# Second layer's modulation moved beside the first feed-forward part, neighbourhood output product between the memory heads, and one split path of probabilities

## The chip, the cores and the metric

The kernel runs on one core of a Trainium2 chip. The metric is the device time of one execution in microseconds (us). Several executions give a median. One execution is also recorded by the hardware profiler, and every duration read below comes from that one.

## What is computed

Two blocks run one after the other on 512 tokens of width 1024, in 32-bit arithmetic. The first mixes three branches (a retention, a neighbourhood attention over an 8 x 64 grid, and a cross attention to 256 memory rows), each gated by a sigmoid of a projection, and ends in a hierarchical mixture of experts. Only the parts that the change touches:

```python
def _memory_cross_attention(xq, mem_n, w_kv):
    mk, mv = jnp.split(mem_n @ w_kv, 2, axis=-1)
    ...
    sc = jnp.einsum('bshd,bmhd->bhsm', q, k).astype(jnp.float32) * (XA_HEAD_DIM ** -0.5)
    p = jax.nn.softmax(sc, axis=-1).astype(v.dtype)
    return jnp.einsum('bhsm,bmhd->bshd', p, v).reshape(b, s, XA_WIDTH)
```

The second block has two layers of attention (latent, differential and grouped heads) and a gated feed-forward part (`silu(h @ gate) * (h @ up) @ down`, inner width 2816). Each layer is modulated: shift, scale and gate are a product of `silu(c)` of two conditioning vectors with a matrix w_ada of 6 x 1024 columns per layer, plus a bias.

## The kernel before, in words

**Precision and weights.** A 32-bit product is made of three products in a rounded format (mm3, lines 97 to 101): high by high, high by low, low by high. A weight tile of 1 MB is loaded by the sync engine's queue (SP) into a tile "raw" of 128 x 2048 (line 70), of which there are NRAW = 3, shared by all that is loaded so. ACT copies it into whi (line 81), DVE subtracts that from raw into wlo (line 82); NW = 3 such pairs exist. `W` does load and split; `ahead` calls it early and keeps the pair. All DMAs of weights stand in SP's queue in program order, and a load waits there until what last read its raw buffer is done.

**The modulation, ada() (lines 1260 to 1327).** A generator over both layers, three rounds each. A round begins with a bias row, loaded into a raw buffer and multiplied by ones; then eight tiles of w_ada follow. Each is loaded into a raw buffer, and four matmuls (32 x 512 outputs, line 1301) read it straight from there, without split. Then come an ACT copy, four transposes and a copy by DVE. `bg()` (line 1329) takes one step of it: it is called after every projection of the first block, in the attention's pairs and after the output products, so that both layers' modulation is done by 658 us.

**First block.** Projections, retention, then the neighbourhood attention in 16 pairs (`pairs`, line 613): scores of two pairs ahead, probabilities turned on PE (prt), product with the values. In the last pairs `ahead` fetches the next weights. `branch_out` (line 491) then makes the branch's output: for each of four 256-wide column groups g a projection to the gate (24 matmuls per half, prj), the product with the branch's output weights (bo), and the gated sum into mixT. For the neighbourhood branch memory_keys runs in the middle of it (mkp, mvp). Then come the memory heads, `pairs` with n = 8 (xs scores, prt turns, xpo products), with a step of ada after each, and their branch_out.

**Attention of the second block (`pipeline`, line 1865).** In 20 units per layer of scores, softmax, turns and products. `turned` transposes normalized probabilities on PE into a PSUM bank tp (three banks of that name) and splits the bank in a high and a low part. SPLITS = (1, 0, 1, 0, 1, 0, 1) says which path each part takes. Path 0: ACT copies from PSUM into pehi, DVE subtracts from PSUM into pelo (line 92). Path 1: ACT copies from PSUM into pe, which is one of the raw buffers for the length of the attention; DVE casts pe to pehi (line 1939), GpSimd subtracts into pelo (line 1940). With six token tiles (layer 0) a unit has seven parts, four on path 1; with four tiles (layer 1) six parts, three on path 1.

**Output projection and feed-forward part.** `attn_out` (line 2002) holds one PSUM bank for each token tile in its first products. `ffn` (line 2055) has 11 groups of inner columns. For each it loads f_gate and f_up, makes 96 products of 512 and, in layer 0, 96 of 256 columns (fg), lets ACT and DVE form the hidden rows (hh, hl), then loads f_down of the group before (`weight(g - 1)`) and makes 72 products (fd) in layer 0, each added by DVE to acc. Layer 0 has six token tiles, layer 1 four.

Of the kernel before, what the change touches and what calls it, by code (L numbers as in the profile page):

```python
# [8 lines left out]
F = mybir.dt.float32  # L9
# [28 lines left out]
class Kern:  # L38
    def __init__(self, tc, ins, outs, stop=None):
        self.tc = tc  # L40
        self.nc = tc.nc
        self.i = ins
        self.o = outs
        self.stop = stop
        self.es = ExitStack()
        self.early = {}


# [138 lines left out]
    def build(self):  # L187
        tc, nc = self.tc, self.nc
        es = self.es
        self.NRAW, self.NW = 3, 3  # L190
        self.cp = es.enter_context(self.pool("consts"))
        self.wp = es.enter_context(self.pool("weights"))
        self.beside = self.ada()
        self.NT5 = 6
        with self.pool("work1") as self.work, self.psum(7, own=dict(ada=1)):
            self.first_block()
            self.bg(100)
# [106 lines left out]
    def proj_b(self, g, evac, after=lambda t: None, before=()):  # L304

        wh, wl = self.w_in(g)

        def product(t):
            p = self.mm("prj")[:, :256]
            for kt in range(8):  # L310
                self.mm3(p, self.h(0, kt, t * 128, t * 128 + 128), self.h(1, kt, t * 128, t * 128 + 128),
                         wh[:, kt], wl[:, kt], kt == 0, kt == 7)
            evac(t, p)

        self.skew(4, *before, product, after)
        self.bg()

# [19 lines left out]
    def retention(self):  # L337
# [108 lines left out]

        nc.sync.dma_start(diff, self.i["posdiff"])
        values(0)
        scores(0)
# [40 lines left out]

    def branch_out(self, yT, nk, wname, gate_group, first=False, middle=lambda: None):

        nc = self.nc
        nw = 2048 // nk
        w = None
        for g in range(4):
            if g == 2:
                middle()
            if g * 256 % nw == 0:
                w = self.W(self.i[wname][g * 256 // nw, 0], k=nk)  # L500

            def evac(f, p, g=g, w=w):
                mx = self.mixT[:, 2 * g + f]
                gt = self.t5("gate")
                nc.scalar.activation(gt, p, AF.Tanh, scale=0.5)
                nc.vector.tensor_scalar(gt, gt, 1.0, 0.5, op0=OP.add, op1=OP.mult)
                py = self.mm("bo")
# [9 lines left out]
            self.proj_a(gate_group + g, evac)  # L517

# [19 lines left out]
    def neighbourhood(self):  # L538
# [53 lines left out]

        self.pairs(16, scores, values, ("w_na_o", (0, 0), 4), ("w_in", (24, 0), 8), ("w_in", (25, 0), 8))
# [4 lines left out]
        oT = self.rows_to_T(o[:, ::-1])  # L598
        self.branch_out(oT, 4, "w_na_o", 24, middle=lambda: self.memory_keys(rows))

# [11 lines left out]

    def pairs(self, n, scores, values, *chunks):

# [4 lines left out]
        for i in range(n + 1):  # L619
# [17 lines left out]
            if i % 2 or n == 8:  # L637
                self.bg()

# [53 lines left out]
    def memory_attention(self):  # L693
# [28 lines left out]

        self.pairs(8, scores, values, ("w_xa_o", (0, 0), 4), ("w_in", (28, 0), 8), ("w_in", (29, 0), 8))
        if self.stop == "xa":
# [535 lines left out]
    def ada(self):  # L1260
# [27 lines left out]
        for l in range(2):  # L1288
# [34 lines left out]
            for nm, g, at in (("a", "g_attn_pre", 8), ("f", "g_ffn_pre", 32)):  # L1323
                t = cp.tile([128, 8, 2], F, name="pre_%s%d" % (nm, l))
                nc.vector.tensor_scalar(t, md[:, at:at + 8], 1.0, None, op0=OP.add)
                nc.vector.tensor_tensor(t, t, self.vec(g, 8 * l, 8)[:, :, None].to_broadcast([128, 8, 2]), op=OP.mult)
                self.preA[nm, l] = t

    def bg(self, n=1):

        for _ in range(n):
            next(self.beside, None)

# [422 lines left out]
    def attention(self, l, yB, ap, nq):  # L1756
# [12 lines left out]
        raw = self.wp.tile([128, 4, 512], F, name="pe", tag="raw", bufs=self.NRAW)  # L1769
        self.copies = [raw[:, j] for j in range(4)]  # L1770

# [87 lines left out]

    SPLITS = (1, 0, 1, 0, 1, 0, 1)
    LAG = 5

    def pipeline(self, units, nq, ap):
# [56 lines left out]
        def turned(u):  # L1922
# [79 lines left out]
    def attn_out(self, l, yB, hT, hp, nq):  # L2002
# [23 lines left out]
        w = weight(0)  # L2026
        ps = [self.mm("wo")[:, :256] for _ in range(nq)]
        for kt in range(8):
            for t in range(nq):
                mms(ps[t], w, t, kt)  # L2030
        for t in range(nq):
# [23 lines left out]
    def ffn(self, l, hT, hp, nq):  # L2055
# [24 lines left out]
        with self.pool("f_w") as fp:  # L2080
            hids, begun = [], []
            for g in range(11):
# [5 lines left out]
                for c0 in range(0, T, N):  # L2088
# [12 lines left out]
                    for f in range(2):  # L2101
# [5 lines left out]
                        self.split(hh[:, c], hl[:, c], sg)  # L2107
                hids.append(hid)
                if 0 < g < 10:
                    wd = weight(g - 1)  # L2110
                    for t in range(nq):
                        down(t, [(hids[g - 1], wd)])
                    begun.append(g)

            parts = [(hids[g], weight(g)) for g in (9, 10)]
# [138 lines left out]
```

## Time and profile before

| | |
|---|---|
| median of 3 executions | 3010.52 us (2999.06 to 3013.27) |
| the profiled execution | 3001.12 us |
| its span (first to last instruction) | 2999.3 us |
| mean granted TensorE clock | 0.975 of full speed |
| PE busy | 2852.1 us |
| DVE busy | 1768.6 us |
| ACT busy | 1296.2 us |
| POOL busy | 413.1 us |

PE is TensorE's matmuls, PEld its weight loads, DVE VectorE, ACT ScalarE, POOL GpSimd, SP the engine that issues the DMAs of weights. Busy time is time in which an instruction of the engine runs. A wait is the engine's idle time ahead of an instruction, put down to what released that instruction last. The time of an execution is the span and some 2 us around it.

### The profile page before, as it was taken

What the parts mean: (1) busy time and instruction counts of PE and PEld (TensorE: products, weight loads), DVE (VectorE), ACT (ScalarE), POOL (GpSimd) and SP (SyncE); (2) the same over time, 40 slices, a digit from 0 to 9 for tenths busy, and PEclk for the clock granted to TensorE, in tenths of its full rate; (3) what the DMA queues carried; (4) which work ended last, traced back from release to release, by engine and by line L of the source; (5) the groups of instructions that cost most, each with busy time, mean ns of one, the idle gap of its engine ahead of it and who ended that gap; (6) DMA issues with size and microseconds to landing.
All of it is one profiled execution on the core that took longest, in us unless ns stands there. A gap on an engine that the chain in (4) does not pass through costs nothing. (4 is left out here: it accounts for less than half of the span.)

```text
span 2999.3 us, 44707 instructions
## 1 busy us (share of the span) xinstructions
PE 2852.1 (95%) x17896; PEld 2463.1 (82%) x17896; DVE 1768.6 (59%) x3239; ACT 1296.2 (43%) x2275; POOL 413.1 (14%) x430
## 2 busy tenths in 40 slices
PE   8999999999799988999999999999988999899998
PEld 6997777769788878887789888888788777888887
DVE  6653344346588877789857343434565787644445
ACT  3222243234477765388745111212342787432222
POOL 2200010000110023156410000000010454000000
PEclk9999999999899999999999999999989999899999
DMA  5443464364799972421013121211233310322221
GB/s 201 141 145 138 150 207 161 142 225 168 262 388 385 351 275 87 146 78 27 4 71 141 71 71 56 71 57 71 77 127 101 106 24 3 141 99 105 92 98 71
DMA packets 130084, 399.78 MB, mean 133 GB/s; under 512 B 62199, under 2 KB 74887, under 8 KB 93128
## 3 DMA queue, kind: packets, MB, share of 16 engines
q1 hardware_dynamic: 116206, 350.04, 32.7%
q0 software_dynamic: 13520, 46.55, 4.6%
q8 instruction: 143, 2.34, 0.3%
q14 instruction: 71, 0.58, 0.1%
q10 hardware_dynamic: 144, 0.26, 0.0%
HBM read 356.64 MB, written 39.39 MB: 132 GB/s over the span
## 5 line engine op out<-in xcount | busy, mean ns | idle before, releaser
L82 DVE TENSOR_TENSOR wlo<-raw,whi 128x2048 fp32r<-128x2048 f32 (+2 forms) x203 | 421.2, 2077 | 292.9 <-ACT whi L81 292.4
L81 ACT ACTIVATE whi<-raw 128x2048 fp32r<-128x2048 f32 (+2 forms) x203 | 351.4, 1739 | 493.7 <-PE fd L101 128.6
L101 PE MATMUL fg<-hT,wlo 128*128 128x512 f32 (+1 forms) x1120 | 386.4, 345 | 0.0
L100 PE MATMUL fg<-hT,whi 128*128 128x512 f32 (+1 forms) x1120 | 386.2, 345 | 0.0
L99 PE MATMUL fg<-hT,whi 128*128 128x512 f32 (+1 forms) x1120 | 386.2, 345 | 0.0
L99 PEld LDWEIGHTS fg<-hT,whi 128*128 128x128 f32 x1120 | 211.1, 189 | 29.3
L100 PEld LDWEIGHTS fg<-hT,whi 128*128 128x128 f32 x1120 | 210.7, 188 | 29.3
L101 PEld LDWEIGHTS fg<-hT,wlo 128*128 128x128 f32 x1120 | 210.8, 188 | 29.0
L1940 POOL TENSOR_TENSOR pelo<-pe,pehi 128x512 fp32r<-128x512 f32 x140 | 181.4, 1298 | 192.0 <-DVE pehi L1939 187.5
L2106 DVE TENSOR_TENSOR sg<-sg,fg 128x512 f32<-128x512 f32 (+1 forms) x70 | 40.1, 573 | 282.1 <-PE fg L101 282.1
L101 PE MATMUL fd<-whi,hl 128*128 128x512 f32 x440 | 173.2, 394 | 0.0
L100 PE MATMUL fd<-wlo,hh 128*128 128x512 f32 x440 | 172.5, 392 | 0.0
L99 PE MATMUL fd<-whi,hh 128*128 128x512 f32 x440 | 171.2, 389 | 0.0
L1903 DVE TENSOR_REDUCE smx<-sn 128x1 f32<-128x768 f32 x160 | 151.8, 950 | 19.1 <-PE sn L1897 18.3
L2073 DVE TENSOR_TENSOR acc<-acc,fd 128x512 f32<-128x512 f32 x180 | 120.8, 686 | 65.1 <-PE fd L101 65.1
L131 PE MATMUL tp<-ident,pn 128*128 128x128 f32 x960 | 150.8, 276 | 4.1 <-DVE pelo L92 2.8
L1906 ACT ACTIVATE pn<-sn,smx 128x768 f32<-128x768 f32 x160 | 144.0, 905 | 19.7 <-DVE smx L1903 16.1
L99 PE MATMUL eg<-whi,xt 128*96 128x256 f32 x512 | 147.0, 287 | 0.0
L100 PE MATMUL eg<-wlo,xt 128*96 128x256 f32 x512 | 145.1, 283 | 1.5 <-DVE wlo L82 1.5
L101 PE MATMUL eg<-whi,xt 128*96 128x256 f32 x512 | 144.9, 283 | 0.0
L82 DVE TENSOR_TENSOR wlo<-rawx,whi 128x2048 fp32r<-128x2048 f32 x58 | 133.0, 2292 | 20.0 <-ACT whi L81 20.0
L1955 PE MATMUL pv<-pehi,vp 128*128 128x512 f32 (+1 forms) x280 | 124.3, 447 | 8.7 <-ACT oT L1959 7.8
(658 smaller groups left out, 7552.0 us busy)
## 6 DMA issues: line engine op xcount, KB each, us to landing
raw<-in_w_in SPq DMA_DIRECT2D x53, 1024.0 KB, 5.3
raw<-in_w_ada SPq DMA_DIRECT2D x48, 1024.0 KB, 5.1
raw<-in_f_gate SPq DMA_DIRECT2D x22, 1024.0 KB, 4.8
raw<-in_f_up SPq DMA_DIRECT2D x22, 1024.0 KB, 4.8
raw<-in_f_down SPq DMA_DIRECT2D x22, 1024.0 KB, 4.8
rawx<-in_e_gate SPq DMA_DIRECT2D x19, 1024.0 KB, 9.1
rawx<-in_e_up SPq DMA_DIRECT2D x19, 1024.0 KB, 9.0
rawx<-in_e_down SPq DMA_DIRECT2D x18, 1024.0 KB, 8.6
```

The source lines that it names most:

```text
L81: keep(nc.scalar.activation(hi[:, c], raw[:, c], AF.Copy))
L82: keep((eng or nc.vector).tensor_tensor(lo[:, c], raw[:, c], hi[:, c].bitcast(F), op=OP.subtract))
L99: t.matmul(ps, lh, rh, start=first, stop=False)
L100: t.matmul(ps, lh, rl, start=False, stop=False)
L101: t.matmul(ps, ll, rh, start=False, stop=last)
L131: self.nc.tensor.transpose(out, in_, self.ident[:k, :k])
L1903: nc.vector.tensor_reduce(m[:, t:t + 1], p[:, :768], axis=AX.X, op=OP.max, negate=True)
L1906: nc.scalar.activation(P[t], p[:, :768], AF.Exp, bias=m[:, t:t + 1], accum_out=su[:, t:t + 1])
L1940: nc.gpsimd.tensor_tensor(el, e, eh.bitcast(F), op=OP.subtract)
L1955: nc.tensor.matmul(p, v[:, k + a], e[:, a * N:a * N + N], start=k == k0 and a == 0 and e is eh, stop=k + a == 5 and e is el)
L2073: nc.vector.tensor_tensor(acc[:, t, cs], acc[:, t, cs], p, op=OP.add)
L2106: nc.vector.tensor_tensor(sg, sg, pp[1], op=OP.mult)
```

## The change

It does five things.

- Layer 1's part of ada() leaves the first block. `bg` counts down from 26 steps, which is layer 0's part, and then does nothing until `second` is set, at layer 0's output projection. In layer 0's ffn two steps follow the products of every even group and three those of every odd one, ahead of f_down's weight; what is left runs after the last group. The products have a PSUM bank of their own, ada, for which the other products' banks go from six to five.
- bg is no longer called in the first projections.
- `branch_out` becomes a generator, branch_steps. The neighbourhood branch's output product is run in 16 steps, two after each of the memory heads' pairs; memory_keys goes ahead of it; the weights fetched in the neighbourhood pairs are w_mem_kv.
- All parts of the probabilities take path 0. pe no longer holds a raw buffer.
- attn_out's first products hold two token tiles in one PSUM bank.

```diff
+    def branch_steps(self, yT, nk, wname, gate_group, first=False):
...
+            wg = self.w_in(gate_group + g)
+            for f in range(2):
+                p = self.mm("prj")
...
+                    self.mm3(p, wg[0][:, kt, fs], wg[1][:, kt, fs], self.h(0, kt), self.h(1, kt), kt == 0, kt == 7)
...
+                yield
+                if f == 1 and g < 3:
+                    self.ahead(("w_in", (gate_group + g + 1, 0), 8))
...
-        self.branch_out(oT, 4, "w_na_o", 24, middle=lambda: self.memory_keys(rows))
+        self.na_out = self.branch_steps(self.rows_to_T(o[:, ::-1]), 4, "w_na_o", 24)
+        self.memory_keys(rows)
...
+        def beside(i):
+            for _ in range(2):
+                next(self.na_out, None)
...
-                with self.pool("l_h") as hp, self.psum(6, own=dict(trp=2)):
+                self.second = True
+                with self.pool("l_h") as hp, self.psum(6 - (l == 0), own=dict(trp=2, ada=1)):
...
         for _ in range(n):
-            next(self.beside, None)
+            if self.layer0 > 0 or self.second:
+                self.layer0 -= 1
+                next(self.beside, None)
...
-                    if self.SPLITS[6 if t0 else k]:
-                        e = self.copies[0]
-                        self.copies.append(self.copies.pop(0))
-                        nc.scalar.activation(e, p, AF.Copy)
-                        nc.vector.tensor_copy(eh, e)
-                        nc.gpsimd.tensor_tensor(el, e, eh.bitcast(F), op=OP.subtract)
-                    else:
-                        self.split(eh, el, p)
+                    self.split(eh, el, p)
...
-        ps = [self.mm("wo")[:, :256] for _ in range(nq)]
+        banks = [self.mm("wo").rearrange("p (a n) -> p a n", a=2) for _ in range(nq // 2)]
+        ps = [banks[t // 2][:, t % 2] for t in range(nq)]
...
+                if l == 0:
+                    self.bg(3 if g % 2 else 2)
                 if 0 < g < 10:
                     wd = weight(g - 1)
```

Three places show how instructions move. Line numbers below 100 are one higher in the changed kernel; its ada loads stand on lines 1319 (bias) and 1324, its products on 1326.

SP's queue in layer 0's feed-forward part, from f_gate of group 1 on, with what each load waits for (a number behind an engine's name is a semaphore's; DMAHW are earlier transfers); before:

```order
L70 DMA raw<-in_f_gate 128x2048 [waits DMAHW4_49,DMAHW6_49,DVE_49,Activation_49]
L70 DMA raw<-in_f_up 128x2048 [waits DMAHW7_49,DVE_49,PE_49]
L70 DMA raw<-in_f_down 128x2048 [waits DMAHW6_49,DMAHW0_49,DVE_49]
L70 DMA raw<-in_f_gate 128x2048 [waits DMAHW1_49,DVE_49,PE_49]
L70 DMA raw<-in_f_up 128x2048 [waits DMAHW7_49,DMAHW2_49,DVE_49]
L70 DMA raw<-in_f_down 128x2048 [waits DMAHW3_49,DMAHW0_49,DVE_49]
L70 DMA raw<-in_f_gate 128x2048 [waits DMAHW1_49,DVE_49]
```

The same place with the change:

```order
L71 DMA raw<-in_f_gate 128x2048 [waits DMAHW6_49,DMAHW3_49,PE_49]
L71 DMA raw<-in_f_up 128x2048 [waits DMAHW7_49,DMAHW4_49,PE_49]
L1324 DMA raw<-in_w_ada 128x2048 [waits DMAHW5_49,DMAHW0_49,PE_49]
L1324 DMA raw<-in_w_ada 128x2048 [waits DMAHW6_49,DVE_49]
L1324 DMA raw<-in_w_ada 128x2048 [waits DMAHW7_49,DMAHW2_49,DVE_49]
L71 DMA raw<-in_f_down 128x2048 [waits DMAHW0_49,PE_49]
L71 DMA raw<-in_f_gate 128x2048 [waits DMAHW1_49,PE_49]
L71 DMA raw<-in_f_up 128x2048 [waits DMAHW2_49,PE_49]
L1324 DMA raw<-in_w_ada 128x2048 [waits DMAHW3_49,DVE_49]
L1324 DMA raw<-in_w_ada 128x2048 [waits DMAHW4_49,DVE_49]
L71 DMA raw<-in_f_down 128x2048 [waits DMAHW5_49,DVE_49]
L71 DMA raw<-in_f_gate 128x2048 [waits DMAHW0_49,DVE_49]
```

Between f_up of a group and f_down of the one before it now stand two or three loads of w_ada, and the first f_down waits for PE.

PE in the same part, at the end of group 1's products, before:

```order
L99 MATMUL fg<-hT_15686,whi 128x256
L100 MATMUL fg<-hT_15687,whi 128x256
L101 MATMUL fg<-hT_15686,wlo 128x256
L99 MATMUL fd<-whi,hh 128x512
L100 MATMUL fd<-wlo,hh 128x512
L101 MATMUL fd<-whi,hl 128x512
```

With the change:

```order
L100 MATMUL fg<-hT_15394,whi 128x256
L101 MATMUL fg<-hT_15395,whi 128x256
L102 MATMUL fg<-hT_15394,wlo 128x256
L1326 MATMUL ada<-raw,silu_c 32x512 x12
L100 MATMUL fd<-whi,hh 128x512 x5
L101 MATMUL fd<-wlo,hh 128x512
L102 MATMUL fd<-whi,hl 128x512
```

Three steps' twelve matmuls stand ahead of f_down's products, of which five with whi now come first.

PE in the memory heads (xs scores, prt turned probabilities, xpo products), before:

```order
L99 MATMUL xs<-mk,xqh 128x256
L100 MATMUL xs<-mk,xqh 128x256
L101 MATMUL xs<-mk,xql 128x256
L131 MATMUL prt<-ident,xpr 128x128 x4
L1301 MATMUL ada<-raw,silu_c 32x512 x3
L719 MATMUL xpo<-mv,prT 128x128 x4
```

With the change:

```order
L102 MATMUL bo<-oTh,wlo 128x512
L100 MATMUL xs<-mk,xqh 128x256
L101 MATMUL xs<-mk,xqh 128x256
L102 MATMUL xs<-mk,xql 128x256
L132 MATMUL prt<-ident,xpr 128x128 x4
L736 MATMUL xpo<-mv,prT 128x128 x4
L100 MATMUL prj<-hTh,whi 128x512
L101 MATMUL prj<-hTl,whi 128x512
L102 MATMUL prj<-hTh,wlo 128x512
```

In place of a step of ada, 24 gate products (prj) and 12 output products (bo) now stand between the heads' pairs.

## Rows read from the trace of the kernel before

**Rows 1.** The page: span, and busy time, share and instructions of each engine.

```profile
span 2999.3 us, 44707 instructions
PE 2852.1 (95%) x17896; PEld 2463.1 (82%) x17896; DVE 1768.6 (59%) x3239; ACT 1296.2 (43%) x2275; POOL 413.1 (14%) x430
```

**Rows 2.** Windows by stage; columns stand in the first row.

```profile
core 0: us, PE busy (x) PEld busy (x) DVE busy (x) ACT busy (x) POOL busy (x), PEclk, DMA share, GB/s
415.00:458.00 43.00, 40.16 (x240) 28.25 (x240) 24.19 (x81) 24.41 (x58) 5.96 (x12) 0.81 0.81 288
584.00:618.00 34.00, 29.83 (x226) 20.57 (x222) 20.52 (x41) 19.92 (x48) 3.57 (x7) 1.00 0.73 263
1290.00:1532.00 242.00, 221.24 (x1530) 190.40 (x1529) 204.03 (x330) 196.36 (x450) 128.00 (x109) 0.99 0.12 34
1660.00:2166.00 506.00, 505.99 (x2685) 431.23 (x2684) 205.09 (x314) 106.49 (x142) 1.59 (x3) 1.00 0.18 62
2335.00:2556.00 221.00, 207.34 (x1332) 169.64 (x1330) 184.68 (x318) 176.21 (x357) 107.17 (x97) 0.99 0.18 48
```

**Rows 3.** Tile ada in 415 to 662 us: records, min/median/max ns, first and last start.

```profile
L1301 PE MATMUL ada<-raw,silu_c x192: 592/617/1062, 420.2 to 656.0; 128*32 128x512 f32 x192
L1296 PE MATMUL ada<-raw,ones x24: 587/600/612, 419.2 to 600.3; 1*32 1x512 f32 x24
L131 PE MATMUL ada<-ident,adar x13: 271/272/273, 414.8 to 658.4; 128*128 128x128 f32 x13
```

**Rows 4.** Timeline, 509.5 to 512 us: start, duration, engine, line, operation.

```profile
509.61 1.06 PE L1296 MATMUL ada<-raw,ones 1*32 1x512 f32 x8
510.60 1.07 PE L1301 MATMUL ada<-raw,silu_c 128*32 128x512 f32 x8
```

**Rows 5.** Waits of PE, 415 to 584 us: in total, times, longest us.

```profile
PE mvp L100 <- DVE wlo L82: 1.5, 1, 1.5
```

**Rows 6.** Waits of PE, 584 to 618 us.

```profile
PE ada L1301 <- DMA raw<-in_w_ada: 4.2, 3, 2.6
```

**Rows 7.** DMA issues, 1660 to 2166 us: KB each, median us to landing.

```profile
raw<-in_f_down SPq DMA_DIRECT2D x9, 1024.0 KB, 4.8
```

**Rows 8.** Groups of ACT and DVE, 1660 to 2166 us: count, busy us, mean ns, idle before.

```profile
L81 ACT ACTIVATE whi<-raw 128x2048 fp32r<-128x2048 f32 x28 | 53.8, 1920 | 149.9 <-PE fd L101 128.6 <-PE fg L100 21.4
L82 DVE TENSOR_TENSOR wlo<-raw,whi 128x2048 fp32r<-128x2048 f32 x28 | 64.1, 2290 | 42.9 <-ACT whi L81 42.9
```

**Rows 9.** Timeline of PE, 1733 to 1735 us: down products.

```profile
1733.75 0.39 PE L99 MATMUL fd<-whi,hh 128*128 128x512 f32 x1
1733.98 0.39 PE L100 MATMUL fd<-wlo,hh 128*128 128x512 f32 x1
```

**Rows 10.** Waits of PE, 1660 to 2180 us.

```profile
PE prj L99 <- ACT whi L81: 5.2, 1, 5.2
```

**Rows 11.** Windows behind that wait; columns as in rows 2.

```profile
2172.00:2174.00 2.00, 1.56 (x7) 1.56 (x8) 0.69 (x1) 1.94 (x4) 0.00 (x0) 0.51 0.06 27
2174.00:2176.00 2.00, 2.00 (x13) 2.00 (x12) 0.94 (x4) 1.48 (x5) 1.56 (x3) 0.64 0.00 0
```

**Rows 12.** Groups of DVE: 1290 to 1532 us first, then 2335 to 2556 us.

```profile
L1939 DVE CAST pehi<-pe 128x512 fp32r<-128x512 f32 x75 | 45.1, 608 | 6.5 <-ACT pe L1938 5.9
L92 DVE TENSOR_TENSOR pelo<-tp,pehi 128x512 fp32r<-128x512 f32 x56 | 38.1, 680 | 2.2 <-ACT pehi L91 2.1
...
L1939 DVE CAST pehi<-pe 128x512 fp32r<-128x512 f32 x60 | 28.1, 468 | 5.8 <-ACT pe L1938 5.2
L92 DVE TENSOR_TENSOR pelo<-tp,pehi 128x512 fp32r<-128x512 f32 x60 | 41.0, 684 | 2.1 <-ACT pehi L91 1.2
```

**Rows 13.** Waits of PE, 1290 to 1532 us.

```profile
PE tp L129 <- DVE pelo L92: 3.3, 3, 1.4
PE tp L131 <- DVE pelo L92: 2.8, 4, 1.0
PE tp L1968 <- DVE pelo L92: 0.8, 2, 0.6
```

More of the change, by code (lines that the diff above doesn't have):

```diff
@@ L46, in __init__ @@
         self.early = {}
+        self.first = True
     def pool(self, name, bufs=1, space=None):
@@ L193, in build @@
         self.beside = self.ada()
+        self.layer0, self.second = 26, False
         self.NT5 = 6
@@ L196, in build @@
             self.first_block()
-            self.bg(100)
+            self.bg(self.layer0)
         if self.stop is None or self.stop[:2] in ("at", "ao", "fo"):
@@ L315, in proj_b @@
         self.skew(4, *before, product, after)
-        self.bg()
+        if not before and not self.first:
+            self.bg()
     def proj_a(self, g, evac):
@@ L447, in retention @@
         nc.sync.dma_start(diff, self.i["posdiff"])
+        self.first = False
         values(0)
@@ L489, in branch_rows, with branch_out @@
         return self.mix[:, 4:6].rearrange("p a (b c) -> p (a b) c", b=2)
-    def branch_out(self, yT, nk, wname, gate_group, first=False, middle=lambda: None):
+    def branch_out(self, *args, **more):
+        for _ in self.branch_steps(*args, **more):
+            pass
+    def branch_steps(self, yT, nk, wname, gate_group, first=False):
         nc = self.nc
@@ L496, in branch_out @@
         for g in range(4):
-            if g == 2:
-                middle()
             if g * 256 % nw == 0:
                 w = self.W(self.i[wname][g * 256 // nw, 0], k=nk)
-            def evac(f, p, g=g, w=w):
-                mx = self.mixT[:, 2 * g + f]
+            wg = self.w_in(gate_group + g)
+            for f in range(2):
+                p = self.mm("prj")
+                fs = slice(f * 128, f * 128 + 128)
+                for kt in range(8):
+                    self.mm3(p, wg[0][:, kt, fs], wg[1][:, kt, fs], self.h(0, kt), self.h(1, kt), kt == 0, kt == 7)
                 gt = self.t5("gate")
@@ L506, in evac @@
                 nc.vector.tensor_scalar(gt, gt, 1.0, 0.5, op0=OP.add, op1=OP.mult)
+                yield
+                if f == 1 and g < 3:
+                    self.ahead(("w_in", (gate_group + g + 1, 0), 8))
+                mx = self.mixT[:, 2 * g + f]
                 py = self.mm("bo")
@@ L516, in evac @@
                     nc.vector.tensor_tensor(mx, mx, gt, op=OP.add)
-            self.proj_a(gate_group + g, evac)
+                yield
+            self.bg()
     def na_table(self):
@@ L591, in values @@
                                     rec[:, :, None].to_broadcast([128, 2, 64]), op=OP.mult)
-        self.pairs(16, scores, values, ("w_na_o", (0, 0), 4), ("w_in", (24, 0), 8), ("w_in", (25, 0), 8))
+        def beside(i):
+            if i % 2:
+                self.bg()
+        self.pairs(16, scores, values, beside, ("w_mem_kv", (0, 0), 8), ("w_mem_kv", (1, 0), 8), ("w_mem_kv", (2, 0), 8))
         if self.stop == "na":
@@ L611, in exps, with pairs @@
         return rec
-    def pairs(self, n, scores, values, *chunks):
+    def pairs(self, n, scores, values, beside, *chunks):
         nc = self.nc
@@ L636, in pairs @@
                 chunks = chunks[1:]
-            if i % 2 or n == 8:
-                self.bg()
+            beside(i)
     def rows_to_T(self, o):
@@ L721, in values, with beside @@
                                     rec[:, :, None].to_broadcast([128, 2, 128]), op=OP.mult)
-        self.pairs(8, scores, values, ("w_xa_o", (0, 0), 4), ("w_in", (28, 0), 8), ("w_in", (29, 0), 8))
+        def beside(i):
+            for _ in range(2):
+                next(self.na_out, None)
+        self.pairs(8, scores, values, beside)
+        for _ in self.na_out:
+            pass
+        self.ahead(("w_xa_o", (0, 0), 4), ("w_in", (28, 0), 8))
         if self.stop == "xa":
@@ L1327, in ada @@
                 self.preA[nm, l] = t
+            yield
     def bg(self, n=1):
         for _ in range(n):
-            next(self.beside, None)
+            if self.layer0 > 0 or self.second:
+                self.layer0 -= 1
+                next(self.beside, None)
     def gates(self, l, which, nq, pool):
@@ L1768, in attention @@
             self.pairs8 += [(hi[:, j], lo[:, j]) for j in range(4)]
-        raw = self.wp.tile([128, 4, 512], F, name="pe", tag="raw", bufs=self.NRAW)
-        self.copies = [raw[:, j] for j in range(4)]
         self.fold = ap.tile([128, 64], F, name="fold")
@@ L1858, in attention @@
             nc.vector.tensor_tensor(y, y, gd[:, None, :].to_broadcast([128, 4, 64]), op=OP.mult)
-    SPLITS = (1, 0, 1, 0, 1, 0, 1)
     LAG = 5
@@ L2026, in attn_out @@
         w = weight(0)
-        ps = [self.mm("wo")[:, :256] for _ in range(nq)]
+        banks = [self.mm("wo").rearrange("p (a n) -> p a n", a=2) for _ in range(nq // 2)]
+        ps = [banks[t // 2][:, t % 2] for t in range(nq)]
         for kt in range(8):
             for t in range(nq):
-                mms(ps[t], w, t, kt)
+                ts = slice(t * 128, t * 128 + 128)
+                for i, (a, b) in enumerate(((0, 0), (0, 1), (1, 0))):
+                    nc.tensor.matmul(ps[t], hT[a][:, kt, ts], w[b][:, kt], start=kt == 0 and t % 2 == 0 and i == 0,
+                                     stop=kt == 7 and i == 2, skip_group_check=True)
         for t in range(nq):
@@ L2113, in ffn @@
                     begun.append(g)
+            if l == 0:
+                self.bg(100)
             parts = [(hids[g], weight(g)) for g in (9, 10)]
```

1 line of the change is left out of this document (removed).

## The prediction

> **What bounds the kernel now.** I read the page's engine shares first [rows 1]: TensorE (PE) is busy 2852.1 of 2999.3 us, 95%, VectorE (DVE) 59%, ScalarE (ACT) 43%, GpSimd (POOL) 14%. So the whole kernel can gain at most some 147 us of PE's idle time and what the clock takes, and work moved from one dense stretch of PE to another costs there what it saves here.
>
> Then the table by stage [rows 2]. Its lines are the stretches on which a term rests: the end of the neighbourhood pairs (415 to 458 us), the memory heads (584 to 618), layer 0's attention (1290 to 1532), layer 0's feed-forward part (1660 to 2166) and layer 1's attention (2335 to 2556). The reader is to see where PE has gaps: 2.84 us in the first (43.00 less 40.16), 4.17 in the second, 20.8 and 13.7 in the attentions. The feed-forward part, which receives the moved work, has none: 505.99 busy of 506.00 us, at DMA share 0.18.
>
> **The second layer's modulation: what leaves.** In 415 to 662 us lie 192 records of modulation products and 24 of bias products [rows 3]. The timeline shows a call's four matmuls as eight records, and the distance from one call to the next [rows 4]: 509.61 to 510.60 and 510.60 to 511.59, so 0.99 us. That makes 24 calls and 3 biases: 27 x 0.99 = 26.7 us; with 12 transposes of about 0.15 (estimate: they overlap, one alone is 0.27 [rows 3]) 28.5 us leave. In the tail of the pairs the calls also filled gaps; I let 2.9 us of the gain be lost there, about as much as is idle now [rows 2]. With the calls go their waits on w_ada, 4.2 us in the memory heads [rows 6], and, as the keys' weights are now fetched ahead, the 1.5 us of the product mvp [rows 5]. **First block: -28.5 + 2.9 - 4.2 - 1.5 = -31.3 us.**
>
> **Where it arrives.** The same 28.5 us are put between products that have no gap: **+28.5**.
>
> **What its loads push.** This is the term that decides. A weight tile lands in one of three raw buffers, is copied by ACT (whi), subtracted by DVE (wlo), and then multiplied. Before, each load waits for a split alone (the SP rows of before end in DVE), and a split is done a whole group of products ahead of its use; PE waits for no weight in 1660 to 2166. The modulation's tiles have no split: PE reads them straight from the raw buffer, so that buffer comes free only when PE has executed the call. In PE's order the calls stand directly ahead of the down products. In the order of SP f_down of group 0 now waits on PE: its buffer is that of the first of the three calls that PE executes just before this very f_down is needed. I followed the buffers of every group: this holds for f_down 0, 2, 4, 5 and 6, and for f_gate 1, which waits for the bias product at the end of group 0; six loads. The other four f_downs (1, 3, 7, 8) wait on a split and stay hidden, and so do the f_gates behind a down product (72 matmuls at 0.23 us [rows 9] are 16 us of cover).
>
> One exposed load: 4.8 us to landing [rows 7], copy 1.92 and subtraction 2.29 [rows 8], 9.0 from trigger to wlo. Meanwhile PE has two further calls (2.0 us); whi comes at 6.7, so PE waits 4.7; then five products with whi alone, at 0.23 us 1.15, then 1.1 more for wlo. **5.9 us.** The trace has such a load already, at the start of layer 1's projections: PE waits 5.2 us for whi [rows 10]. After it the granted clock is 0.51 in one stretch of 2 us, 0.64 in the next, and then full [rows 11]; of 1.56 and 2.00 us busy that takes 1.56 x 0.49 + 2.00 x 0.36 = 1.5 us. I take half of it, 0.8, since here the stall is cut in two by products and PE is dense before; the bounds are nothing and 1.5. Six loads at 6.7: **+40.2** (35 to 44).
>
> **The probabilities.** 140 parts change path, 80 in layer 0 and 60 in layer 1 (four of seven and three of six in 20 units; the trace has records of 75 and 60 [rows 12]). Gone are 140 casts on DVE and 140 subtractions on POOL; added are 140 subtractions on DVE from PSUM, as those that exist. ACT keeps one copy. DVE: 80 x (680 - 608) ns + 60 x (684 - 468) ns = 5.8 + 13.0 = 18.7 us more, in stages where it is busy 204.03 of 242.00 and 184.68 of 221.00 [rows 2]. The subtraction holds a PSUM bank of tp, of which there are three, where path one released it after ACT's copy; PE's waits on "DVE pelo" are 3.3, 2.8 and 0.8 us [rows 13], all on such banks. Two bounds: those 6.9 us grow with the number of parts held, by 140/60 times or some +9; and the waits shrink by up to 10 of the 34 idle us, since every part has one hand-over less (ACT to DVE instead of ACT to DVE to POOL, which is busy 128.00 of 242.00 us [rows 2]). I take **+3**, nearer to the first, whose wait the trace shows.
>
> The Trainium skill (VectorE: DVE Perf Modes, The TRN2 errata, and The perf-mode tier table) speaks against this part: a 32-bit copy within SBUF may run at twice the rate, a two-tensor operation may not, and one that reads PSUM has the dearer fixed cost; by its cycle row 327 ns become 658, an estimate of 46 us more on DVE over 140 parts. The rows put the cast at 608 and 468 ns, so the trace agrees in direction and not in size. The skill's SBUF page (SBUF — State Buffer, Who interferes with whom) names a reason: such a copy shares a port pair with GpSimd, and the later one blocks; the traces so far show no such cast without POOL beside it.
>
> **Output product between memory heads, output projection, start.** The same matmuls in another order: the memory heads' waits on ACT and DVE are covered by 24 gate products and 12 output products at a time in place of the four of a call. Beyond the waits counted above there is nothing to gain there; a w_in tile that comes late would cost one 5.9 us. Zero, with +6 as a bound. Pairing two token tiles in a bank leaves the matmuls as they were: zero. The first calls of the modulation come later, with the same count in the first block: zero.
>
> **Sum.** -31.3 + 28.5 + 40.2 + 3 = +40.4 us on the profiled execution's 3001.1 (its span stands in [rows 1]): **3042 us**, 1% above the median of the runs shown, 3010.5, which itself is 9.4 above the profiled one.
>
> **Rivals.**
> 1. *The loads stay hidden.* If PE's way from the trigger to the product were 9 us instead of 3, or the transfer started at another event than I read, nothing would be exposed: 3001.1 - 31.3 + 28.5 + 3 = **3001**, not slower; with the attention's better bound 2988. For it speaks DMA's low share (0.18). Against it: the share says nothing of when a transfer may begin, and the order has the calls next to the down products. It decides at 3.1 + 5.9 = 9.0 us of PE work between the call and the product.
> 2. *VectorE bounds the attentions.* All 18.7 us come out on PE, since DVE is at 84% there and the bank is held through it: 3042 - 3 + 18.7 = **3058**. The 6.9 us speak for it, against it that PE's other waits are on ACT. By the skill's 46 us it would be 3085; I give that no chance of its own, because the casts' rows are far above its 327 ns.
> 3. *Attention relieved.* The shorter hand-over and DVE without POOL beside it: -10 instead of +3, **3029**. Both casts' means, 608 beside more POOL work and 468 beside less, speak for it.
> 4. *The change of order doesn't do what it says:* the modulation's loads are so late that calls run only at the end of the part, in bg(100). Then three buffers turn at 4.8 us each, 1.6 us a call, 38 us for the 24 in place of 28.5 + 40.2: **3011**. The counters in the code give 2 or 3 calls a group, and the order shows them there, so I leave it at a few in a hundred.
>
> **The numbers.** Forecast 0.55, own range 3030 to 3056 (stall 35 to 44, attention -2 to +9, order 0 to +6); rival 1 0.17, rival 2 0.14, rival 3 0.10, rival 4 0.04. A measurement of this kernel tells 0.5% from no change, 15 us, so the limits are 2995.5 and 3025.6. Faster: a third of rival 1, 0.06. Same: the rest of it, rival 4 and a fifth of rival 3, 0.17. Slower: 0.77. For 8 in 10 the range begins at 3010, leaving out most of rival 1, and ends at 3070, which takes in rival 2 with its spread.
>
> **What would show it.** Right: in the feed-forward part of layer 0 PE waits for whi before fd five times and before fg once, 4 to 5 us each, and for wlo near 1 us behind it; the part from f_gate 0 to the last down some 69 us longer than 506; in the first block no ada row after layer 0's, the block 31 us shorter; CAST pehi gone, all 260 subtractions pelo on DVE, POOL about 180 us less. Wrong, if the waits on whi are absent there (rival 1), if they are above 8 us each, or if the attentions' lengths move by more than 10 us.

## The result, and the profile after

The changed kernel takes 3026.36 us (median of 8 executions, 3021.07 to 3036.17), the kernel before 2998.07 us (8 executions, 2990.13 to 3013.27). The ratio is 1.0085, with a 95% interval of 1.0063 to 1.0108. By that ratio it is some 25 us slower, as it is in the two profiled executions (3001.12 and 3026.24 us); the medians lie 28 us apart. The forecast was 3042 us, the range 3010 to 3070, slower the likely side.

The page of the changed kernel, with its span and the engines' busy time, against [rows 1]:

```profile
span 3024.5 us, 44636 instructions
PE 2858.2 (95%) x17896; PEld 2478.5 (82%) x17896; DVE 1766.0 (58%) x3239; ACT 1296.5 (43%) x2275; POOL 226.3 (7%) x290
```

PE has the same 17896 matmuls and 6 us more of busy time; GpSimd lost 187 us of work. The span grew by 25.2 us. The next table shows where. Its boundaries are first starts of matmuls in the two traces: the first score product (sn) of a layer, the first product of the output projection (wo) of a layer, the last down product.

| stretch, us | before | after | difference |
|---|---|---|---|
| start to the first sn of layer 0 (first block, mixture of experts, first projections) | 1261.2 | 1224.3 | -36.9 |
| layer 0's attention, first sn to first wo | 272.8 | 260.8 | -12.0 |
| layer 0's output projection, feed-forward part, layer 1's projections | 800.1 | 877.3 | +77.2 |
| layer 1's attention | 224.4 | 219.5 | -4.9 |
| layer 1's rest to the last down product | 430.8 | 432.5 | +1.7 |

In the third stretch, the piece from the first gate product (fg) to the first projection of layer 1 went from 559.6 to 635.6 us, +76.0. PE's waits there are these; before, none was for a weight of this part, and the one of the projection behind it [rows 10] is unchanged at 5.2 us. Columns are total us, times, longest:

```profile
PE fd L100 <- ACT whi L82: 21.9, 5, 5.3
PE fg L100 <- ACT whi L82: 4.9, 1, 4.9
PE ada L132 <- ACT adar L1330: 1.4, 2, 0.7
PE ada L1326 <- DMA raw<-in_w_ada: 1.3, 1, 1.3
PE fg L102 <- DVE wlo L83: 1.1, 1, 1.1
```

Five times fd and once fg wait for whi, as the order of the loads said; the timeline puts them at f_gate 1 and f_down 0, 2, 4, 5 and 6. The load of f_down 0 is issued at 1647.74 us, behind the first of the calls, which PE begins at 1646.62. The loads themselves were hardly slower than the 4.8 us of [rows 7]; here are their KB and the median us from issue to landing in this part:

```profile
raw<-in_f_down SPq DMA_DIRECT2D x11, 1024.0 KB, 5.0
```

The stretch around f_down 0, in windows of 2 us with the columns of [rows 2]:

```profile
1650.00:1652.00 2.00, 0.00 (x0) 0.00 (x0) 0.00 (x0) 0.00 (x0) 0.00 (x0) 1.00 1.02 422
1652.00:1654.00 2.00, 0.00 (x0) 0.00 (x0) 0.00 (x0) 1.41 (x1) 0.00 (x0) 0.76 1.00 422
1654.00:1656.00 2.00, 1.45 (x3) 1.17 (x4) 1.47 (x1) 1.41 (x2) 0.00 (x0) 0.50 1.02 430
1656.00:1658.00 2.00, 2.00 (x6) 1.26 (x5) 1.79 (x2) 1.39 (x2) 0.00 (x0) 0.50 0.65 205
1658.00:1660.00 2.00, 2.00 (x7) 1.57 (x6) 1.91 (x2) 1.53 (x1) 0.00 (x0) 0.53 0.81 299
1660.00:1662.00 2.00, 2.00 (x10) 1.66 (x9) 0.80 (x2) 0.00 (x0) 0.00 (x0) 1.00 1.00 389
```

PE stands idle while DMA is at its full share (1.00 to 1.02); then, from 1654 on, PE is busy at the lower of its two clock levels, 1.2 GHz (0.50), for over 5 us before 2.4 GHz are granted again. That takes 1.45 x 0.50 + 2.00 x 0.50 + 2.00 x 0.47 = 2.7 us of work. The same windows behind the other five waits show 0.50 for 4 to 6 us of busy time too; worked out in this way the six lose 2.1 to 3.1 us each, 15.7 us in all. In the kernel before, this part has 1.00 throughout [rows 2].

Layer 0's attention, PE's waits after, against [rows 13]:

```profile
PE sn L1920 <- ACT pn L1929: 3.1, 10, 0.4
PE pv L1971 <- ACT oT L1975: 0.9, 1, 0.9
PE tp L132 <- DVE pelo L93: 0.5, 2, 0.3
```

VectorE there: the subtraction that all parts now have, two casts of other tiles, and a subtraction of two inputs in SBUF (line 1883):

```profile
L93 DVE TENSOR_TENSOR pelo<-tp,pehi 128x512 fp32r<-128x512 f32 x131 | 88.4, 684 | 7.1 <-ACT pehi L92 6.5
L1826 DVE CAST dqst<-dqrow 128x384 fp32r<-128x384 f32 x8 | 3.2, 397 | 0.0
L1863 DVE CAST gqst<-gqr 128x384 fp32r<-128x384 f32 x8 | 2.7, 348 | 0.0
L1883 DVE TENSOR_TENSOR yB<-yB,dif_y 128x256 f32<-128x256 f32 x6 | 2.4, 413 | 0.0
```

The last three in the kernel before, over the whole of that attention:

```profile
L1800 DVE CAST dqst<-dqrow 128x384 fp32r<-128x384 f32 x8 | 5.1, 634 | 3.0 <-PE tp L129 3.0
L1837 DVE CAST gqst<-gqr 128x384 fp32r<-128x384 f32 x8 | 3.9, 487 | 0.8 <-issue 0.8
L1857 DVE TENSOR_TENSOR yB<-yB,dif_y 128x256 f32<-128x256 f32 x6 | 5.1, 864 | 0.0
```

The subtraction pelo costs what it did (680 ns in [rows 12]), but the other three, which the change does not touch, went from 634 to 397, from 487 to 348 and from 864 to 413 ns. These are the windows of layer 0's and layer 1's attention, against 204.03 of 242.00 and 184.68 of 221.00 us of VectorE in [rows 2]:

```profile
1253.00:1484.00 231.00, 220.94 (x1537) 191.83 (x1536) 199.77 (x333) 196.00 (x451) 28.27 (x35) 1.00 0.11 28
2360.00:2580.00 220.00, 206.50 (x1352) 172.70 (x1350) 189.28 (x320) 177.72 (x358) 27.91 (x37) 1.00 0.16 41
```

VectorE's work went down by some 4 us in layer 0 and up by some 5 in layer 1. Over the whole of both attentions, first sn to first wo, it is 411.5 us in either kernel.

### The profile page after: what moved, and what is told of

Read it like the earlier page. It is cut to its first block, busy times and chain, and to the rows that moved or that the text cites. A ratio compares the mean times of both kernels' runs of the same rounds, so it can differ in the third digit from the quotient of the medians.

```text
span 3024.5 us, 44636 instructions
## 1 busy us (share of the span) xinstructions
PE 2858.2 (95%) x17896; PEld 2478.5 (82%) x17896; DVE 1766.0 (58%) x3239; ACT 1296.5 (43%) x2275; POOL 226.3 (7%) x290
## 5 line engine op out<-in xcount | busy, mean ns | idle before, releaser
L101 PEld LDWEIGHTS fg<-hT,whi 128*128 128x128 f32 x1120 | 211.2, 189 | 29.9
L100 PE MATMUL fd<-whi,hh 128*128 128x512 f32 x440 | 177.6, 413 | 21.9 <-ACT whi L82 21.9
L93 DVE TENSOR_TENSOR pelo<-tp,pehi 128x512 fp32r<-128x512 f32 x260 | 175.2, 683 | 13.9 <-ACT pehi L92 11.9
L92 ACT ACTIVATE pehi<-tp 128x512 fp32r<-128x512 f32 x260 | 154.2, 602 | 43.8 <-PE tp L132 42.3
```

The source lines that it names most:

```text
L92: nc.scalar.activation(hi, src, AF.Copy)
L93: nc.vector.tensor_tensor(lo, src, hi.bitcast(F), op=OP.subtract)
L100: t.matmul(ps, lh, rh, start=first, stop=False)
L101: t.matmul(ps, lh, rl, start=False, stop=False)
```

## Experiments

Four questions are at stake: whether the loads that stand bare in the feed-forward part are the loss; whether the modulation's leaving is the first block's whole gain; whether one path shortens the attentions by itself, and by what; whether the output product between the memory heads gives something. Medians of before differ by a few us from one set of runs to the next (2998 to 3004), so each ratio is to runs of before on the same chip.

**One path of probabilities alone**, in the kernel before, with pe's raw buffer kept:

```diff
-    SPLITS = (1, 0, 1, 0, 1, 0, 1)
+    SPLITS = (0, 0, 0, 0, 0, 0, 0)
```

> Before, with every part of the probabilities on path 0; the buffer pe stays reserved, nothing else moves. Theory A (the attentions got shorter because VectorE's operations no longer meet GpSimd's subtractions and a part has one hand-over less): layer 0's attention about 11 us shorter, layer 1's 2 us, in all 2998 - 13 = 2985 us, ratio 0.996; PE's waits on DVE pelo go from 6.9 to below 1 us. Theory B (they got shorter because pe gave its raw buffer back and weights came earlier): no change, 2998 us. Theory C (the prediction's: VectorE has 19 us more to do and tp's banks are held): 3001 us or more.

2988.95 us, ratio 0.9957 (0.9942 to 0.9973). Layer 0's attention took 262.7 us in place of 272.8, layer 1's 222.2 in place of 224.4. PE's waits in layer 0's attention:

```profile
PE sn L1897 <- ACT pn L1906: 4.4, 12, 0.7
PE tp L131 <- DVE pelo L92: 1.0, 3, 0.5
```

The gain of 13 us comes from the path itself, not from the buffer, and the prediction's sign (theory C) is refuted. The total rests on the medians: the profiled execution is 17 us above its median, and the first block takes that (last section). The two parts of theory A, GpSimd's absence and the hand-over that is gone, are not told apart here.

**The modulation moved alone.** The kernel before with all of the change that touches ada, bg, the banks and the pairs of tiles in a bank; the edit is cut to its core:

```diff
+                if l == 0:
+                    self.bg(3 if g % 2 else 2)
                 if 0 < g < 10:
                     wd = weight(g - 1)
```

> Before, with the second layer's modulation moved alone (and the two token tiles in a bank that its bank of PSUM needs). Theory A (six loads of weights stand bare in layer 0's feed-forward part, and the low clock behind each costs some 3 us more): that part 75 us longer, the first block 30 us shorter, 2998 + 45 = 3043 us, ratio 1.015. Theory B (the first block's gain of 38 us in the changed kernel is due to the modulation's leaving alone, none of it to the output product): 2998 + 75 - 38 = 3035 us, ratio 1.012.

3036.84 us, ratio 1.0123 (1.0102 to 1.0143), which is 37 us more. The stretch to the first sn is 1226.9 us, 34.3 less; the piece from fg to the projections 635.5, 75.9 more, with the same waits:

```profile
PE fd L100 <- ACT whi L82: 21.6, 5, 5.2
```

So the move alone costs more than the whole change, and the other parts give some of it back. Of the first block's gain of 37 us, 34 are the modulation's alone; the total is theory B's, 1.012.

**The output product between the memory heads alone**, in the kernel before, with a step of the modulation kept behind each pair:

```diff
+        def beside(i):
+            for _ in range(2):
+                next(self.na_out, None)
+            self.bg()
...
+        self.pairs(8, scores, values, beside)
```

> Before, with the neighbourhood output product between the memory heads' pairs alone; one step of the modulation stays behind each pair. Theory A (the product fills waits of the memory heads and of the keys' weights that the modulation filled too, but not all): 4 to 8 us less, 2992 us, ratio 0.998. Theory B (without the modulation's leaving it gives nothing, as its loads and the gates' weights meet in the three raw buffers): 2998 us or some more.

3006.72 us, ratio 1.0015 (0.9997 to 1.0033): no gain. The waits on w_ada are gone, but one for a gate's weight has come, in 450 to 720 us:

```profile
PE prj L99 <- ACT whi L81: 4.7, 1, 4.7
```

Theory A, that it fills waits, fails in this form: a late weight took the place of the late modulation tiles. That the product costs something isn't shown either: the interval contains 1, and of the 6.5 us by which this profiled execution is the longer one, 2.8 lie ahead of the first sn. Layer 0's feed-forward part, which the edit does not touch, took 6.8 us more (566.4 us); two further kernels that leave it alone show nearly as much (566.3 and 564.3).

**The change without the modulation's move**, the changed kernel with the calls as before:

```diff
-            if self.layer0 > 0 or self.second:
-                self.layer0 -= 1
-                next(self.beside, None)
+            next(self.beside, None)
...
             for _ in range(2):
                 next(self.na_out, None)
+            self.bg()
...
-                if l == 0:
-                    self.bg(3 if g % 2 else 2)
```

> The changed kernel with the modulation back in the first block, wholly as before (its calls also behind each memory pair). Theory A (the modulation's place is the whole loss, 43 us or so, and the other parts gain): 3026 - 43 = 2983 us, ratio to before 0.994 to 0.996. Theory B (the modulation's place costs only the 38 us of the feed-forward part that its leaving did not give back): 2988 us. Theory C (the other parts do not gain by themselves): 2998 us.

2994.24 us, ratio 0.9983 (0.9966 to 0.9999). That lies between theories B and C: the other parts gain, but less than the attentions alone promised. In its trace these are 16.4 us shorter (261.3 and 219.5 us) and the stretch to the first sn is 9.7 us longer (1270.9); the granted clock there is 0.50 from 430 to 460 us, as in the last section, so what the output product has to do with it isn't shown. The parts add up all the same: the ratios of the path and of the product alone give 0.9957 x 1.0015 = 0.9972, within the interval, and with the modulation's 1.0123 it is 1.0095, where the whole change has 1.0085.

**Asking for f_down first.** In the changed kernel, one line moved:

```diff
+                if 0 < g < 10:
+                    wd = weight(g - 1)
                 if l == 0:
                     self.bg(3 if g % 2 else 2)
                 if 0 < g < 10:
-                    wd = weight(g - 1)
                     for t in range(nq):
```

> The changed kernel with f_down's weight asked for ahead of the group's modulation calls instead of behind them; everything else as it is. Theory A (the loads wait for calls that PE runs just before the product; asked for earlier, f_down's buffer comes free a whole group ahead, only f_gate of group 1 still waits for the end of group 0): five of the six waits of 3 to 5 us go, with the 2.7 us that the low clock takes behind each: 3026 - 25 - 13 = 2988 us, ratio to before 0.996. Theory B (the transfers meet each other: w_ada's 24 MB in this part hold back f_down whatever the order): waits of the same sum on f_gate, f_up or w_ada, 3020 us or more, ratio 1.007 or more.

2985.48 us, ratio 0.9942 (0.9922 to 0.9961). All five waits of fd are gone, and the piece from fg to the projections takes 595.3 us in place of 635.6; of the waits for weights in the feed-forward part there stay

```profile
PE fg L100 <- ACT whi L82: 4.9, 1, 4.9
PE fg L102 <- DVE wlo L83: 1.1, 1, 1.1
```

which are f_gate of group 1. Theory B, transfers that hinder each other, would have kept waits of the same sum, but the same 24 MB now cross the same part unnoticed. What cost the time was when the loads could start.

**And no call in group 0**, three in each of groups 1 to 9; shown against the run above:

```diff
-                if l == 0:
-                    self.bg(3 if g % 2 else 2)
+                if l == 0 and 0 < g < 10:
+                    self.bg(3)
```

> As the one above, and the calls begin in group 1 with three in each, none in group 0. Theory A: the sixth wait goes too, no wait of PE on whi in the feed-forward part, which is then some 28.5 us longer than before (559.6 + 28.5 = 588 us): 3026 - 31 - 16 = 2979 us, ratio to before 0.993 to 0.994. Theory B: 3020 us or more.

2981.93 us, ratio 0.992 (0.9899 to 0.9941): 24 us faster than before, and 1.6% less than the change as made (0.992 / 1.0085). With the run above, this is what shows that the six loads are the loss. No wait on a weight is left between fg and the projections, that piece takes 589.5 us, and the part reads, with the columns of [rows 2],

```profile
1560.00:2140.00 580.00, 578.94 (x3280) 480.32 (x3279) 237.08 (x394) 134.07 (x192) 7.31 (x13) 1.00 0.31 113
```

busy 578.94 of 580.00 us at full clock. 589.5 - 559.6 = 29.9 us is what the moved products themselves cost, where the sum had 28.5.

**The same without the output product between the heads**, which also keeps pe's raw buffer; the edit is shown against the run above, cut to its core:

```diff
-        self.na_out = self.branch_steps(self.rows_to_T(o[:, ::-1]), 4, "w_na_o", 24)
-        self.memory_keys(rows)
+        oT = self.rows_to_T(o[:, ::-1])
+        self.branch_out(oT, 4, "w_na_o", 24, middle=lambda: self.memory_keys(rows))
```

> The one above with the neighbourhood output product where it was before, so: the modulation moved and its loads hidden, one path of probabilities, nothing else. Theory A (the output product between the memory heads gives nothing, or costs the 4 us that the run of it alone showed): 2976 us, ratio 0.992, the same as the one above or some less. Theory B (with the modulation gone the memory heads need that product as cover): 6 to 10 us above the one above, 2987 us.

2981.46 us, ratio 0.9918 (0.9896 to 0.9941): the same. The output product's place is worth nothing once the modulation's tiles have left (the stretch to the first sn is 1228.0 us, 1227.8 with it).

**GpSimd beside one path.** The kernel of one path alone, with 140 subtractions on GpSimd that have no reader:

```diff
+    SPLITS = (0, 0, 0, 0, 0, 0, 0)
...
                         self.split(eh, el, p)
+                        if (1, 0, 1, 0, 1, 0, 1)[6 if t0 else k]:
+                            nc.gpsimd.tensor_tensor(self.copies[1], self.copies[0], eh.bitcast(F), op=OP.subtract)
```

> Before with one path of probabilities, and for each part that was on path 1 a GpSimd subtraction that reads pehi and a scratch tile and whose result nobody uses (140, as many as before the change). Theory A (the attentions' gain is that VectorE's casts no longer meet GpSimd): layer 0's attention goes back from 262 towards 272 us, the casts dqst, dkst and gqst from 350 to 400 ns back to 500 to 700 ns, total 2994 us, ratio above 0.997. Theory B (the gain is the shorter hand-over and the cast that is gone, GpSimd's presence is of no matter): layer 0's attention stays at 260 to 264 us, 2987 us, ratio 0.996.

2991.59 us, ratio 0.9965 (0.9949 to 0.9981), which cannot be told from 0.9957. GpSimd is as busy in layer 0's attention as before (136.6 us against 139.1). That attention is 265.9 us (262.7 with one path alone, 272.8 before), and some waits on pelo are back:

```profile
PE tp L131 <- DVE pelo L92: 3.1, 6, 1.0
```

VectorE's groups over the whole of that attention:

```profile
L92 DVE TENSOR_TENSOR pelo<-tp,pehi 128x512 fp32r<-128x512 f32 x140 | 94.4, 682 | 6.7 <-ACT pehi L91 6.1
L1801 DVE CAST dqst<-dqrow 128x384 fp32r<-128x384 f32 x8 | 3.4, 427 | 0.0
L1838 DVE CAST gqst<-gqr 128x384 fp32r<-128x384 f32 x8 | 3.8, 488 | 0.0
L1858 DVE TENSOR_TENSOR yB<-yB,dif_y 128x256 f32<-128x256 f32 x6 | 3.9, 656 | 0.0
```

The casts take 427 and 488 ns in place of 397 and 348, the subtraction within SBUF 656 in place of 413; the subtraction that reads PSUM keeps its 682. So GpSimd's presence lengthens some of VectorE's operations within SBUF and gives back 3 of layer 0's 10 us (that attention took 260.8 to 262.7 us in the six kernels with one path and no such work on GpSimd). In layer 1 it gives back none (220.8 us, against 222.2 with one path alone). Neither theory is right alone, and the other 7 us, which would be the cast pehi that is gone and the shorter hand-over, were not tried apart.

**Path 1 for all parts**, in the kernel before:

```diff
-    SPLITS = (1, 0, 1, 0, 1, 0, 1)
+    SPLITS = (1, 1, 1, 1, 1, 1, 1)
```

> Before with every part of the probabilities on path 1: 280 parts' cast on VectorE and subtraction on GpSimd in place of 140; the reverse of the change's step. Theory A (path 1 costs, by its longer hand-over and by GpSimd beside VectorE's copies): layer 0's attention 280 us or more (272.8 before, 262.7 with path 0 alone), total 3010 us, ratio above 1.003. Theory B (the prediction's: path 0 costs, as it holds a bank of tp through VectorE's subtraction, and its subtraction is the longer one on VectorE): the waits on pelo go and layer 0's attention is 268 us or less, ratio below 0.998.

There are 260 parts, not 280: seven in each of 20 units in layer 0, six in layer 1.

3052.31 us, ratio 1.016 (1.014 to 1.018). Layer 0's attention is 296.4 us, layer 1's 253.3, together 52.5 more than before. The casts on VectorE in layer 0's attention:

```profile
L1939 DVE CAST pehi<-pe 128x512 fp32r<-128x512 f32 x135 | 102.0, 770 | 5.7 <-ACT pe L1938 5.2
L1800 DVE CAST dqst<-dqrow 128x384 fp32r<-128x384 f32 x8 | 7.2, 902 | 0.3 <-PE tp L129 0.3
L1837 DVE CAST gqst<-gqr 128x384 fp32r<-128x384 f32 x8 | 6.9, 864 | 0.0
```

Two of PE's waits that grew there, and what the scores' wait is in its turn waiting for:

```profile
PE sn L1897 <- ACT pn L1906: 22.0, 13, 3.4
PE pv L1955 <- POOL pelo L1940: 3.1, 4, 1.5
ACT pn L1906 <- DVE smx L1903: 23.1, 21, 3.5
```

The cast pehi takes 770 ns here, more than the 684 of the subtraction that replaces it in the changed kernel, and dqst 902 ns, against 397 without path 1. No wait on pelo of VectorE is left, as theory B said of the banks; but the scores now wait 22.0 us in place of 4.9, behind an ACT that waits for VectorE. The granted clock is 0.93 and 0.95 in the two attentions, where before it is 0.98 in both; by PE's busy time there (258.8 and 216.1 us against 248.4 and 210.1) that is an estimated 20 of the 52.5 us. Theory A holds, and more strongly than its figure.

## Why the prediction was right, and where not

*What leaves the first block: -31.3 predicted.* Measured are -34.3 with the modulation alone and -36.9 in the whole change, against one execution of before; three other kernels whose first block is that of before took 1264.6, 1266.5 and 1278.0 us to the first sn, not 1261.2. The direction holds, and the size as far as one execution of each can tell, but the terms inside came out otherwise. The windows up to the first sn, before and after, and a wait that is new after:

```profile
0.00:1261.20 1261.20, 1196.93 (x8005) 1031.11 (x8005) 758.54 (x1379) 552.94 (x826) 143.40 (x181) 0.97 0.58 210
0.00:1224.30 1224.30, 1159.92 (x7776) 1028.30 (x7776) 749.83 (x1368) 550.12 (x823) 139.54 (x174) 0.97 0.54 198
PE trp L132 <- DVE xr L680: 4.4, 1, 4.4
```

PE's idle time is 64.3 and 64.4 us: the waits on w_ada went, and a transposition of the memory rows now waits for VectorE. The gain is all in PE's busy time, 37.0 us where the sum had 28.5. Why the calls took more there than they cost in the feed-forward part isn't shown; that the sum came within 3 to 6 us is luck in part.

*What arrives: +28.5.* With the loads hidden it is 29.9 us and 28.4 us in the two kernels of the repaired order (589.5 and 588.0 less 559.6). Right, within what single executions differ by: kernels that leave this part alone took 558.8 to 566.4 us for it.

*What its loads push: six loads, 6.7 us each, 40.2.* The six were the right ones, each found by the buffer that it waits for. The part took 554.0 us before, from f_gate 0 to the last down (the 506 of the prediction is a window within it), and grew by 76.0. Measured: 76.0 - 28.5 = 47.5, above the bound of 44. The waits are shorter than taken: with those on the modulation's own tiles and copies they are 21.9 + 4.9 + 1.4 + 1.3 + 1.1 = 30.6 us, against 6 x 5.9 = 35.4. The mis-sized term is the clock: "I take half of it, 0.8" was too little, and its upper bound of 1.5 too; each wait is followed by 2.6 us of lost work in the mean, 15.7 in all (30.6 + 15.7 + 28.5 = 74.8 of the 76.0 us). In the rows that I took it from [rows 11] the low clock ends 3 us after the wait; in the six places PE was busy for 4 to 6 us at it. At half clock the five products of f_down 0 take 2.3 us in place of 1.15, as long as the subtraction of wlo (2.29). So the second wait, for wlo, appears once in place of six times: the clock's loss covers it.

*The probabilities: +3 (-2 to +9).* Wrong in sign: -12.0 and -4.9 us in the two attentions, and -13 for the whole with this part alone. (Kernels with one path read 260.8 to 262.7 and 219.5 to 222.2 us there, so of the -4.9 some 2.7 can be spread.) The prediction's own sign of being wrong, an attention that moves by more than 10 us, was met in layer 0. The step that failed is "those 6.9 us grow with the number of parts held": they fell to 0.5 us with 140 parts held in place of 60. And the 18.7 us more of VectorE work did not come: 411.5 us in both kernels. The sum priced the cast by its own rows, 608 and 468 ns, and the other operations of the stage not at all; these got shorter as path 1 left and longer with all parts on it. GpSimd beside them is part of the reason, 3 of 10 us in layer 0; the rest is open. That path 0 holds the bank stays true of the code, but no wait here grew by it. Rival 3, which had 0.10, is what happened here in direction, and went further than its -10.

The Trainium skill (VectorE: DVE Perf Modes, The TRN2 errata) gave the estimate of 46 us more of VectorE work. The trace shows none of it, and no mean of the pehi casts of these runs, 468 to 770 ns, came near that estimate's 327 ns.

The Trainium skill (SBUF — State Buffer, Who interferes with whom) says that a copy in the two-port mode and GpSimd shut each other out, while an operation with at most one input in SBUF, outside that mode, does not meet GpSimd. The trace agrees on the second: the subtraction from PSUM takes 682 to 684 ns with GpSimd beside it or not. On the first it agrees in direction, by dqst and gqst; but GpSimd's load alone does not set the time, since pehi took 608 and 468 ns beside a GpSimd that was busy 128.00 of 242.00 and 107.17 of 221.00 us [rows 2].

*Output product, output projection: zero.* The output product is right for the pair of kernels with the loads hidden (0.992 and 0.9918); alone, with the modulation in the block, it brought one late weight of 4.7 us, within the +6 allowed. The output projection with two tiles in a bank took 78.8 us before and 79.2 after, first wo to first fg.

*The total.* Of the sum's +40.4 the first block took 5.6 us more away, the feed-forward part added 7.3 us more, the attentions were 19.9 us less, and the stretches outside them 2.9 us more: 40.4 - 5.6 + 7.3 - 19.9 + 2.9 = 25.1 us, on 3001.1 some 3026. The largest error is that of the attentions. 3026 us lies outside the forecast's own range, 3030 to 3056, and inside the wider one, 3010 to 3070. That forecast and measurement are only 15 us apart is luck in part: the first block and the attentions came out 25.5 us lower than the sum, and the loads and the stretches outside 10.2 us higher. The direction rested on the six loads, and held: with them gone the change is a gain.

## What to carry to other kernels

A tile that an engine reads straight from a shared load buffer frees the buffer only when that engine has run; the next load in that buffer then starts behind that engine's own order. Before moving such a consumer, follow the buffers in rotation to see whose load inherits them, and ask first for what is needed first: one line moved here turned 25 us lost into 17 gained (ratio 1.0085 into 0.9942). And when a removed operation shares a port or an engine with others, price the others too.

## What was not expected of the hardware

An exposed load cost its wait and half as much again here: behind waits of 2.8 to 5.3 us the granted clock stood at 0.50 for some 4 to 6 us of busy time in each of six places, 15.7 us on 30.6 us of waits.

The second finding concerns the spread between executions. The instructions of PE up to the attention are the same in the kernel before and in the one with one path alone, yet the last of the neighbourhood scores (ns) started at 442.6 us in one profiled execution and at 456.8 in the other. The windows of the kernel before, with the columns of [rows 2]:

```profile
420.00:430.00 10.00, 10.00 (x66) 6.10 (x63) 5.38 (x24) 5.74 (x14) 1.13 (x2) 1.00 0.72 257
430.00:440.00 10.00, 10.00 (x73) 7.35 (x71) 7.01 (x22) 7.29 (x18) 0.00 (x0) 1.00 0.93 328
440.00:450.00 10.00, 7.16 (x31) 4.58 (x31) 5.26 (x14) 4.53 (x11) 3.71 (x7) 0.57 0.79 264
```

and of the kernel with one path alone:

```profile
410.00:420.00 10.00, 10.00 (x73) 7.07 (x72) 6.90 (x30) 5.02 (x16) 2.58 (x5) 0.99 0.50 176
420.00:430.00 10.00, 10.00 (x32) 5.64 (x30) 2.38 (x12) 2.31 (x7) 0.57 (x1) 0.50 0.71 244
430.00:440.00 10.00, 10.00 (x42) 7.15 (x41) 5.38 (x15) 4.75 (x11) 0.56 (x1) 0.50 0.47 149
440.00:450.00 10.00, 10.00 (x37) 5.66 (x37) 2.88 (x12) 3.46 (x7) 0.00 (x0) 0.50 0.42 123
```

The clock went to 0.50 at 420 us, behind stretches in which PE was busy 10.00 of 10.00 us, and stayed there while PE was busy. The change without the modulation's move shows the same from 423 us on. In the kernel before the clock falls some 20 us later, in the gaps of the pairs' tail. What decides was not tried. One execution can carry some 14 us of it, so the verdicts above rest on medians. The first line of the table by stretch compares executions whose pairs' last scores started within 4 us of each other (442.6 and 439.0).
